# Seven block products instead of eight for the values and gates of a retention layer, inside a two-layer decoder trunk

## The chip, the cores and the metric

The kernel runs on one core of a Trainium2 chip. Times are device microseconds of one execution, the median of several runs where not said otherwise; the profile is of one profiled execution. TensorE does the matrix products, VectorE, ScalarE and GpSimd the elementwise work, and SyncE issues the transfers. In the profile these are PE (PEld its weight loads), DVE, ACT, POOL and SP.

## The reference

A residual stream `h` of 1024 tokens by 1024 features passes two layers. Everything is float32.

```python
u = rms_norm(x, ret_norm_pre)
q, k, v, g = split(u @ ret_w_in)          # 4 heads: q, k of 256, v, g of 512 features
q, k = rope(q), rope(k) / 16
o = retention(q, k, v)                    # o_t = sum_{s<=t} gamma_h^(t-s) (q_t.k_s) v_s
o = (o - mean(o)) * rsqrt(var(o) + EPS)   # per head and token
h = x + rms_norm((o * silu(g)) @ ret_w_out, ret_norm_post)
k2, v2 = split(rms_norm(h, kv_norm) @ w_kv)          # 8 heads: k of 128, v of 256
q2, g2 = split(rms_norm(h, sb_norm_pre) @ sb_w_in)
o2 = stick_breaking_attention(q2, k2, v2)
out = h + rms_norm((o2 * silu(g2)) @ sb_w_out, sb_norm_post)
```

## The kernel before

**Layout.** Features lie on the 128 partitions, tokens along the free side. The tokens are worked through in two halves of 512. `run()` (L691) goes through four phases: retention on half 0 and half 1 (A, t = 0 and 1), then attention on half 0 and half 1 (C). Each phase has four units: the retention heads, or pairs of attention heads. The state of each retention head after half 0 goes through DRAM (`st_d`) to half 1; keys and values of attention half 0 do too.

**Precision.** Each float32 operand is split in two parts of a reduced matmul type: a rounded copy (ScalarE) and the remainder (VectorE). A product is then three matmuls, high by high, high by low and low by high (`mm3`, L114). An operand of activations is 128 x 2 x 512 (`hl`).

**Weights.** They lie in DRAM as units of 128 x 1024 (512 KB). `unit` (L91) loads one into a raw tile `wraw` (three buffers), copies it (L107) and subtracts (L108) into `whl` (three buffers). Where a gain belongs to it, L110 and L111 do that with the gain of the norm as a scale. A projection (`proj`, L119) of 1024 features by 512 columns takes 4 units and 96 matmuls: 8 row blocks, 4 PSUM banks, 3 matmuls each; a unit serves 24 matmuls. Type "N" leaves features on the partitions (q, k), type "V" keeps the tokens' block as the stationary operand and streams the weights, so that tokens are on the partitions (v, g).

**One retention unit** (`AHead`, L289): the projection of q and k, in which the previous head's gate is done as side steps; the output projection of the previous head (`outproj`, L145); the projection of v, with the scores as side steps; the projection of g, with the mix as side steps (scores times v, plus the state; normalised per token; `mix`). The `rope` step (L278) reads each of the four banks of q and k twice on VectorE, adds on GpSimd and splits. The pre-norm factor of each token isn't applied to x: x is split with the gain only (L255, L256), the sums of squares run beside it, and the factor is put into the cosine and sine tables, into a scale of v (L303, L307, L308) and of g (L317, L318).

**What becomes of y.** The output projection sums over the heads: `y` lives in SBUF as eight tiles of 128 x 512, each chunk copied (first head, L164) or added (L166), and with the last head squared and summed (`sumsq`, L185, its additions on GpSimd at L191). `a_post` (L418), which runs as side steps of the next phase's first two units, takes the row of factors, scales y, adds x, splits h and stores it twice: in split form (`hh_d`) and whole (`h_d`). `c_prep` loads the split form for the attention phases; there too the token factor is multiplied in after the projections (L487 for keys and queries, L505 for values, L516 for gates), and the gate's last multiplication is on GpSimd (L518). `c_post` scales y, adds h (into a table tile of two buffers) and stores the result; `finish` is the last output projection of the kernel, with the closing norm.

**The order of the work.** `merge` (L172) deals the side steps out among the chunks of a projection; a scheduler then sets the order on each engine, and pools of tiles with a fixed number of buffers bring the waits. PSUM has eight banks: four "mm" (projections), two "z" (scores, transposes, sums), two "o" (mix, first two chunks of a retention output projection). All transfers are issued by SyncE (L61), in one queue that runs in order.

## Time and profile before

| | before |
|---|---|
| median of three runs | 1817.19 us (1815.28, 1817.19, 1819.95) |
| profiled execution | 1819.82 us, span 1818.0 us, mean TensorE clock 0.993 |
| busy TensorE, VectorE, ScalarE, GpSimd | 1767.5, 1038.1, 724.1, 308.6 us |
| bytes moved by DMA | 208.09 MB, 114 GB/s on average |
| retention half 0, half 1 (last addition to y of each) | 0 to some 442 us, then to some 875 us |
| attention half 0, half 1 | then to some 1293 us, then to the end |

A row of groups reads: line, engine, operation, output <- inputs, shapes, count, then busy us and mean ns of one, then the idle time of its engine just before and what ended it. A row of windows reads: the stretch in us, its length, and for PE, PEld, DVE, ACT and POOL the busy us with the number of instructions, then the TensorE clock granted, the DMA share and GB/s. A matmul's busy time is not the spacing of matmuls, since they overlap. A row of waits reads: engine and line that waited, what released it, us in all, times, longest.

### The profile page before, as it was taken

Reading aid. Unit: us, or ns where it says so; the run is one execution under the profiler, and the core shown is the slowest. Engines: PE = TensorE matmul, PEld = TensorE weight load, DVE = VectorE, ACT = ScalarE, POOL = GpSimd, SP = SyncE. Lnnn points to the kernel's source line nnn. Section 1 sums busy time; section 2 is a strip of 40 time slices with the busy share of each in tenths; the row PEclk is TensorE's granted clock in tenths of the full one; section 3 lists DMA queues with packets and bytes.
Section 4 is the critical chain, followed back from the end, with each engine's and each line's share of the span. In section 5 each row is a group of like instructions: output and inputs, shape, how many; then the busy total and the mean of one; then the engine's idle time right before and its main releaser. Section 6 shows DMA issues by size and latency. Waiting matters only on the chain.

```text
span 1818.0 us, 21852 instructions
## 1 busy us (share of the span) xinstructions
PE 1767.5 (97%) x8290; PEld 1466.5 (81%) x8290; DVE 1038.1 (57%) x1588; ACT 724.1 (40%) x1288; POOL 308.6 (17%) x376
## 2 busy tenths in 40 slices
PE   7999999999899999999999999999998999999987
PEld 6888888888788888888877888888876887887876
DVE  7363454564945363545596465556586446756665
ACT  4343323353333232323454343443444434444441
POOL 4110010113431010111122120201212012101123
PEclk9999999999999999999999999999999999999999
DMA  5222222343362232243364423354244232222321
GB/s 175 82 94 92 93 82 92 108 158 105 136 212 93 70 105 92 83 147 108 116 245 172 140 72 127 115 180 133 99 133 134 87 105 93 92 82 91 108 79 49
DMA packets 66376, 208.09 MB, mean 114 GB/s; under 512 B 7520, under 2 KB 9696, under 8 KB 66272
## 3 DMA queue, kind: packets, MB, share of 16 engines
q1 hardware_dynamic: 66272, 206.70, 33.9%
q8 instruction: 65, 1.06, 0.2%
q14 instruction: 39, 0.32, 0.1%
HBM read 173.12 MB, written 33.55 MB: 114 GB/s over the span
## 4 chain that ended last, share of the span: by engine, by line
PE 71%; issue 17%; DVE 7%; POOL 2%; DMA 2%; ACT 1%; SPq 0%; POOLq 0%; DVEq 0%; ACTq 0%
PE pmm L115 19%; PE pmm L117 19%; PE pmm L116 19%; PE po L117 3%; PE po L116 3%; PE po L115 3%; DVE sgn L550 2%; DMA tab<-h 1%; DVE whl L111 1%; PE pz L117 1%; PE pz L116 1%; PE pz L415 1%; PE pz L115 1%; PE pz L575 1%; DVE A L551 1%
## 5 line engine op out<-in xcount | busy, mean ns | idle before, releaser
L108 DVE TENSOR_TENSOR whl<-wraw,whl 128x1024 fp32r<-128x1024 f32 (+1 forms) x158 | 196.6, 1246 | 217.6 <-ACT whl L107 217.3
L115 PE MATMUL pmm<-xh,whl 128*128 128x512 f32 x768 | 308.3, 401 | 11.5 <-ACT whl L107 7.3
L115 PE MATMUL pmm<-whl,xh 128*128 128x512 f32 x768 | 302.1, 394 | 4.1 <-DVE v L308 2.7
L117 PE MATMUL pmm<-xh,whl 128*128 128x512 f32 x768 | 301.9, 393 | 0.7 <-DVE whl L108 0.7
L116 PE MATMUL pmm<-xh,whl 128*128 128x512 f32 x768 | 300.9, 392 | 0.0
L116 PE MATMUL pmm<-whl,xh 128*128 128x512 f32 x768 | 300.3, 391 | 0.0
L117 PE MATMUL pmm<-whl,xh 128*128 128x512 f32 x768 | 300.3, 391 | 0.0
L107 ACT ACTIVATE whl<-wraw 128x1024 fp32r<-128x1024 f32 (+1 forms) x158 | 165.3, 1047 | 237.9 <-PE pmm L117 225.6
L111 DVE SCALAR_TENSOR_TENSOR whl<-wraw,gn,whl 128x256 fp32r<-128x256 f32 (+1 forms) x256 | 153.2, 639 | 103.5 <-ACT whl L110 103.0
L110 ACT ACTIVATE whl<-wraw,gn 128x256 fp32r<-128x256 f32 (+1 forms) x256 | 143.7, 608 | 148.7 <-PE pmm L117 111.0
L115 PEld LDWEIGHTS pmm<-xh,whl 128*128 128x128 f32 x768 | 145.3, 189 | 41.4 <-ACT whl L107 7.3
L115 PEld LDWEIGHTS pmm<-whl,xh 128*128 128x128 f32 x768 | 144.9, 189 | 34.1 <-DVE v L308 2.9
L117 PEld LDWEIGHTS pmm<-xh,whl 128*128 128x128 f32 x768 | 144.8, 189 | 33.5 <-DVE whl L108 1.7
L117 PEld LDWEIGHTS pmm<-whl,xh 128*128 128x128 f32 x768 | 144.7, 188 | 30.8
L116 PEld LDWEIGHTS pmm<-whl,xh 128*128 128x128 f32 x768 | 145.0, 189 | 28.3
L116 PEld LDWEIGHTS pmm<-xh,whl 128*128 128x128 f32 x768 | 145.3, 189 | 26.6
L548 POOL TENSOR_SCALAR_AFFINE_SELECT sgn<-sgn 128x128 f32<-128x128 f32 x64 | 24.9, 389 | 638.8 <-ACT sgn L543 603.0
L115 PE MATMUL pmm<-oT,whl 128*128 128x512 f32 x336 | 132.9, 395 | 0.0
L117 PE MATMUL pmm<-oT,whl 128*128 128x512 f32 x336 | 131.5, 391 | 0.0
L116 PE MATMUL pmm<-oT,whl 128*128 128x512 f32 x336 | 131.4, 391 | 0.0
L550 DVE TENSOR_TENSOR_SCAN sgn<-sgn 128x128 f32<-128x128 f32 (+3 forms) x64 | 92.7, 1448 | 58.8 <-POOL sgn L548 58.8
L191 POOL TENSOR_TENSOR acc<-acc,f 128x512 f32<-128x512 f32 x49 | 74.4, 1522 | 147.5 <-ACT f L190 146.6
(182 smaller groups left out, 2822.5 us busy)
## 6 DMA issues: line engine op xcount, KB each, us to landing
wraw<-in_wts_dram SPq DMA_DIRECT2D x254, 512.0 KB, 3.3
xh<-hh SPq DMA_DIRECT2D x16, 512.0 KB, 3.7
v<-v SPq DMA_DIRECT2D x16, 512.0 KB, 3.2
vo<-v SPq DMA_DIRECT2D x32, 256.0 KB, 3.2
st<-ko SPq DMA_DIRECT2D x8, 512.0 KB, 3.6
vo<-in_xT_dram SPq DMA_DIRECT2D x16, 256.0 KB, 5.1
ko<-st SPq DMA_DIRECT2D x8, 512.0 KB, 3.9
h<-y SPq DMA_DIRECT2D x16, 256.0 KB, 2.7
```

The source lines that it names most:

```text
L107: A_.activation(w[:, 0, a:b], raw[:, a:b], AF.Copy)
L108: V.tensor_tensor(w[:, 1, a:b], raw[:, a:b], f32(w[:, 0, a:b]), ALU.subtract)
L110: A_.activation(w[:, 0, a:b], raw[:, a:b], AF.Copy, scale=g)
L111: V.scalar_tensor_tensor(w[:, 1, a:b], raw[:, a:b], g, f32(w[:, 0, a:b]), ALU.mult, ALU.subtract)
L115: MM(p, lh, rh, start=start, stop=False)
L116: MM(p, lh, rl, start=False, stop=False)
L117: MM(p, ll, rh, start=False, stop=stop)
L191: G.tensor_tensor(acc[:], acc[:], t[:], ALU.add)
L415: nc.tensor.transpose(pt[:, 128 * e:128 * e + 128], on[:, 128 * e:128 * e + 128], ident[:])
L548: G.affine_select(n[:, dg], n[:, dg], [[-1, 128]], ALU.is_gt, 1.0, base=0, channel_multiplier=1)
L550: V.tensor_tensor_scan(n[:, :W][:, ::-1], n[:, :W][:, ::-1], n[:, :W][:, ::-1], 1.0, ALU.mult, ALU.bypass)
L551: V.tensor_tensor(a[:, :W - 1], a[:, :W - 1], n[:, 1:W], ALU.mult)
```

## The change

**Seven products.** For one head and one half, v and g are [v g] = x W with W of 1024 by 1024 and x of 512 tokens. Cut into two by two blocks (two token halves of 256, two feature halves of 512 on the one side; v and g on the other) this is eight block products and four sums. The new `vg` computes it in seven products, with four sums of blocks on either side and a few on the results (a Strassen-Winograd form). The blocks of x are combined once per half (`sums`, four operands `T`, split like x); the blocks of W are combined for each head in `left`: 16 raw units are loaded instead of 8, and 14 are split, of which 8 are sums or differences first made on VectorE in place or in a new tile `S` (two buffers). A unit serves 12 matmuls. The products accumulate in two pairs of banks, `ma` and `mb`: a product may continue on the bank of the one before it (`goes_on`), after that has been copied to an SBUF tile (`copy`, ScalarE) or added to such a copy (`plus`, VectorE). This is done for every head of both halves but the first of half 0, which keeps two projections, v from x without the token factor (`first_v`) and g from normed x.

**Norm first.** x and h are multiplied by the token factor before they are split, so rotary tables, v, g and all attention evacuations lose their factor. `a_stats` takes the statistics of half 1 during half 0 (steps `pre`, dealt out at u = 2 and again at u = 3 of the first phase). In attention the gate's last multiplication moves from GpSimd to VectorE, reading PSUM.

**y in DRAM.** Each chunk of an output projection loads its y from DRAM, adds and stores it (`y_d`). `a_post` stores h once, whole; `c_prep` loads that, multiplies and splits. `a_post` is moved from the first unit of the next retention phase to its second and third. `f2` has six buffers instead of five, the scores have tiles of their own, and the four "mm" banks are two `ma` and two `mb`, which projections and output projections take in the order `banks4`.

```diff
-    BUFS = dict(xh=8, y=8, tab=2, wraw=3, whl=3, qk=4, v=4, vo=4, oT=4, A=5, sgn=2, AT=3,
-                ko=2, sg=4, row=1, f2=5, acc=2, small=24, col=8, mm=4, z=2, o=2)
+    BUFS = dict(xh=8, tab=2, wraw=3, whl=3, S=2, qk=4, v=4, vo=4, oT=4, A=5, sgn=2, AT=3,
+                ko=2, sg=4, f2=6, acc=2, small=24, col=8, sc0=1, sc1=1, sc2=1, sc3=1, ma=2, mb=2, z=2, o=2)
+    banks4 = ("mb", "mb", "ma", "ma")
...
-                box["p"] = PS(tag if c < 2 else "mm")
+                box["p"] = PS(tag if tag and c < 2 else banks4[c % 4])
+                box["y"] = S("f2", [512])
+                if not first:
+                    dma(box["y"][:], y_d[c])
...
-                V.tensor_tensor(y[c][:], p[:], y[c][:], ALU.add)
+                V.tensor_tensor(y[:], p[:], y[:], ALU.add)
+            dma(y_d[c], y[:])
...
+            V.scalar_tensor_tensor(src, src, gcol(G_PRE, k), X.row[:], ALU.mult, ALU.mult)
+            x = X.xh[k] = hl("xh")
+            split((x[:, 0, :], x[:, 1, :]), src)
...
+            V.tensor_tensor(a[:, 0], q[1], q[0], ALU.subtract)
+            V.tensor_tensor(a[:, 1], q[3], a[:, 0], ALU.subtract)
+            V.tensor_tensor(b[:, 0], q[3], q[1], ALU.subtract)
+            V.tensor_tensor(b[:, 1], q[2], a[:, 1], ALU.subtract)
...
+            def left(n, i):
+                s = box["S"]
+                if n == 1:
+                    src = load(0, i)
+                elif n == 2:
+                    src = load(0, 2 + i)
+                elif n == 5:
+                    a, b = load(1, i), load(1, 2 + i)
+                    src = s[i] = S("S", [1024])
+                    V.tensor_tensor(src[:], a[:], b[:], ALU.add)
+                elif n == 6:
+                    a, src = load(0, i), s[i]
+                    V.tensor_tensor(src[:], src[:], a[:], ALU.subtract)
+                elif n == 3:
+                    src = load(0, 2 + i)
+                    V.tensor_tensor(src[:], src[:], s[i][:], ALU.subtract)
+                elif n == 7:
+                    a, src = load(1, 2 + i), s[i]
+                    V.tensor_tensor(src[:], a[:], src[:], ALU.subtract)
+                else:
+                    src = load(1, 2 + i)
+                w = S("whl", [2, 1024], F32R)
+                split((w[:, 0, :], w[:, 1, :]), src[:])
+                return w
...
+            order = [(n, i) for n in (1, 2, 5, 6, 3, 7, 4) for i in range(2)]
...
+                banks = box["be"] if n in (2, 5, 3) else box["al"]
+                first = n in (1, 2, 5)
+                for tb in range(2):
+                    xh, xl = right(n, kt, tb)
+                    cl = slice(512 * kk, 512 * kk + 512)
+                    mm3(banks[tb][:], xh, xl, w[:, 0, cl], w[:, 1, cl], first and kt == 0, kt == 3, goes_on=not first)
+                if kt < 3:
+                    return
+                for tb, p in enumerate(banks):
+                    if n in (1, 5, 6):
+                        box[n, tb] = copy(p)
+                    elif n == 2:
+                        self.vput(tb, plus(box[1, tb], p), cc[:, 4 * h + tb:4 * h + tb + 1])
+                    elif n == 3:
+                        self.vput(2 + tb, plus(box[6, tb], p), cc[:, 4 * h + 2 + tb:4 * h + 3 + tb])
+                    elif n == 7:
+                        self.gput(2 + tb, plus(box[5, tb], p))
+                    else:
+                        self.gput(tb, p[:])
...
-                    merge(H.vproj(), (H.scores(), 7, 0), (post3[0] if u == 0 else post3[3] if u == 1 else [], 0, 0))
-                    merge(H.gproj(), (H.mix(), 3, 0), (post3[1] if u == 0 else [], 4, 0))
+                        merge(held if u < 3 else held[:4], (pre if u == 2 and nxt[0] == "A" else post[:4] if u == 1 else post[6:9] if u == 2 else pre, 0, 2 if u < 3 else 0))
...
+                    mix = H.mix()
+                    n = 3 if t else 2
+                    side = [(H.scores(), 7, 11), (mix[:n], 14, 6), (mix[n:n + 2], 23, 0)]
+                    if u in (1, 2):
+                        side.append((post[4:6] if u == 1 else post[9:], 4, 8))
+                    merge(H.vg(), *side)
+                    rest = mix[n + 2:]
```

More of the change, by code (lines that the diff above doesn't have):

```diff
@@ new lines, in stat1, with a_stats, sq, col @@
+        def stat1():
+            tables()
+            first.col = rstd_col(first.acc)
+        def stat2():
+            X.row = keep_row(first.col)
+        return X, first, [lambda k=k: load(k) for k in range(8)], \
+            [stat1, stat2] + [lambda k=k: norm(k) for k in range(8)], [lambda i=i: sums(i) for i in range(4)]
+    def a_stats(t):
+        box = {}
+        def sq(i):
+            raw = a_load(t, i, "wraw")
+            A_.activation(raw[:], raw[:], AF.Square)
+            if i == 0:
+                box["acc"] = S("acc", [512])
+                G.tensor_tensor(box["acc"][:], raw[:, 0:512], raw[:, 512:1024], ALU.add)
+            else:
+                for c in range(2):
+                    G.tensor_tensor(box["acc"][:], box["acc"][:], raw[:, 512 * c:512 * c + 512], ALU.add)
+        def col():
+            box["col"] = rstd_col(box["acc"])
+        def row():
+            rowh[0] = keep_row(box["col"])
+        return [lambda i=i: sq(i) for i in range(4)] + [col, row]
@@ L325, in scores, with out @@
+        def out(self, y_d, acc=None):
+            return outproj(self.base + 12, self.oT, y_d, self.h == 0, acc, "o")
         def scores(self):
@@ L639, in prep, with fetch @@
             hs.append(a)
+        def fetch():
+            for ng in range(4):
+                f = S("oT", [2, 512])
+                for b in range(2):
+                    dma(f[:, b], y_d[2 * ng + b])
+                    y.append(f[:, b])
         def chunk(th, c):
@@ L747, in run @@
                     last = P
-            acc = S("acc", [512])
             if kind == "A":
-                side = (last.gate(), 1, 4)
+                side = (rest + last.gate(), 1, 4)
             else:
```

335 lines of the change are left out of this document (195 added, 140 removed).

## The prediction

> **What bounds the kernel now.** First the page's list of engines and its chain of waits: where is the end set?
>
> ```profile
> span 1818.0 us, 21852 instructions
> PE 1767.5 (97%) x8290; PEld 1466.5 (81%) x8290; DVE 1038.1 (57%) x1588; ACT 724.1 (40%) x1288; POOL 308.6 (17%) x376
> PE 71%; issue 17%; DVE 7%; POOL 2%; DMA 2%; ACT 1%; SPq 0%; POOLq 0%; DVEq 0%; ACTq 0%
> ```
>
> TensorE is busy 97% of the span, VectorE 57%. Busy is not the price of a matmul, though. The grouped rows give the busy mean, the timeline of TensorE the spacing:
>
> ```profile
> L116 PE MATMUL pmm<-xh,whl 128*128 128x512 f32 x768 | 300.9, 392 | 0.0
> 300.22 0.39 PE L117 MATMUL pmm<-whl,xh 128*128 128x512 f32 x1
> 300.45 0.39 PE L115 MATMUL pmm<-whl,xh 128*128 128x512 f32 x1
> ...
> 309.29 0.39 PE L115 MATMUL po<-v,vo 128*128 128x512 f32 x1
> 317.45 0.60 PE L415 MATMUL pz<-ident,sgn 128*128 128x128 f32 x4
> ```
>
> Each matmul shows 0.39 us, but they overlap: from the one at 300.22 to the one at 309.29 lie 40 of them, all of this width, 9.07 / 40 = 0.2268 us from start to start. So a removed 512-wide matmul returns 0.2268 us, not 0.392. (Four 128-wide transposes take 0.60, 0.15 each.) The Trainium skill, Perfetto Trace Analysis, section Identifying the Most-Contended Engine, says the same: matmul busy time is a poor measure as matmuls overlap, and the weight loads' share is the better one; here that is 81% against 97%.
>
> Next, windows of the four phases, where idle time of TensorE would show (columns: window, us, then PE, PEld, DVE, ACT, POOL busy, TensorE clock, DMA share, GB/s):
>
> ```profile
> 0.00:10.00 10.00, 2.69 (x6) 2.10 (x7) 3.29 (x8) 4.91 (x8) 1.22 (x5) 1.00 0.65 198
> 100.00:200.00 100.00, 100.00 (x466) 83.09 (x465) 42.10 (x66) 36.98 (x61) 10.68 (x16) 1.00 0.27 89
> 490.00:500.00 10.00, 4.47 (x17) 3.29 (x16) 10.00 (x12) 2.95 (x5) 4.17 (x4) 0.80 0.60 184
> 970.00:980.00 10.00, 8.10 (x28) 6.68 (x29) 2.94 (x6) 0.66 (x2) 0.00 (x0) 0.66 0.76 286
> 1500.00:1600.00 100.00, 97.90 (x456) 80.48 (x456) 67.04 (x86) 46.51 (x87) 16.18 (x20) 1.00 0.28 90
> ```
>
> In most of a retention half TensorE never idles; its holes are at the start (7 us), where the post of a half stands in the first unit of the next (5.5 us near 490, with VectorE full; 1.9 near 970, with a clock of 0.66) and some 2% of the attention halves. Retention is a pure matmul count, so matmuls taken out there pay in full, as long as what feeds them keeps up.
>
> **The change, part by part.** *Matmuls.* Seven of the eight (head, half) units run 7 x 2 x 12 = 168 matmuls of 512 for values and gates instead of 192: 7 x 24 = 168 fewer. 168 x 0.2268 = **-38.1 us**. (By busy means it would be -65.7; I don't take that.)
>
> *What feeds them.* A weight unit used to carry 24 matmuls (5.44 us), now 12 (2.72 us), and 8 of the 14 are first combined on VectorE. Prices:
>
> ```profile
> wraw<-in_wts_dram SPq DMA_DIRECT2D x254, 512.0 KB, 3.3
> L107 ACT ACTIVATE whl<-wraw 128x1024 fp32r<-128x1024 f32 x154 | 163.0, 1058 | 237.0 <-PE pmm L117 225.6 <-issue 8.4 <-PE po L117 2.8
> L108 DVE TENSOR_TENSOR whl<-wraw,whl 128x1024 fp32r<-128x1024 f32 x154 | 193.6, 1257 | 217.3 <-ACT whl L107 217.0
> 469.40 1.93 DVE L108 TENSOR_TENSOR whl<-wraw,whl 128x1024 fp32r<-128x1024 f32 x1
> 477.60 1.21 DVE L108 TENSOR_TENSOR whl<-wraw,whl 128x1024 fp32r<-128x1024 f32 x1
> 478.74 3.11 DVE L438 SCALAR_TENSOR_TENSOR y<-y,gn,row 128x512 f32<-128x512 f32 x3
> L166 DVE TENSOR_TENSOR y<-pmm,y 128x512 f32<-128x512 f32 x76 | 52.1, 686 | 51.3 <-PE pmm L117 51.3
> L308 DVE SCALAR_TENSOR_TENSOR v<-pmm,small,v 128x512 fp32r<-128x512 f32 x32 | 22.7, 749 | 15.6 <-ACT v L307 15.6
> ```
>
> A 1024-wide subtraction occupies VectorE 1.14 us (477.60 to 478.74), 1.26 by the mean, 1.93 beside GpSimd work. One vg stage needs 14 splits + 8 combinations = 22 x 1.14 = 25.1, 6 additions of a copied product and 8 evacuations at some 0.63 = 8.8, and the splits of the scores (1280 columns) and of the first outputs, some 4.9 (an estimate from 0.69 per 512 columns): 38.8 us; with the mean durations 45. TensorE has 168 x 0.2268 = 38.1 there (by chance the saving's number too), and as side steps 24 score matmuls of 320 columns on average (3.4), 16 transposes (2.4) and 30 matmuls of the mix (6.8): 50.7 us. So VectorE runs at 77 to 89% and TensorE still leads. A unit's chain, 3.3 + 1.26 + 1.06 + 1.26 = 6.9 us, starts one unit ahead and three raw buffers deep; it is hidden in the mean, not at each handoff: the second load of product 5 and the load of product 7 can only be issued when a raw buffer comes free, with some 3 us to spare before their unit is due.
>
> The Trainium skill, SBUF — State Buffer, section Who interferes with whom, states that a VectorE instruction with two SBUF inputs contends with a GpSimd one that reads SBUF; the 1.93 against 1.21 above agrees, and speaks against this change, whose combinations all have two SBUF inputs. By it, were all eight combinations of a stage to meet one, VectorE would have 8 x 0.72 = 5.8 us more, 44.6 of 50.7: an estimate that leaves the sum alone and feeds the slower rival's chance.
>
> Direct waits stay in each stage: product 5 takes the bank pair of product 2, and product 4 continues on the pair of product 7, so TensorE waits until an addition (0.69) has read the bank. The later bank's own three matmuls (0.68) hide about half: 0.5 to 1 us each. I take 2 us a stage, **+14** over seven; lower end 0, upper end 6 a stage (VectorE at its mean durations, each handoff late).
>
> *Banks.* The rotary step now leaves k in "ma", and chunk 2 of the output projection asks for "ma" first; before, it got the first bank freed.
>
> ```profile
> L280 DVE TENSOR_TENSOR f<-pmm,tab 128x512 f32<-128x512 f32 x16 | 10.9, 679 | 1.0 <-PE pmm L117 1.0
> 462.31 0.69 DVE L280 TENSOR_TENSOR f<-pmm,tab 128x512 f32<-128x512 f32 x1 [0.98 <-PE pmm L117]
> 462.91 0.68 DVE L281 TENSOR_TENSOR f<-pmm,tab 128x512 f32<-128x512 f32 x1
> ```
>
> That bank is free after six reads, 6 x 0.60 = 3.6, with two splits of 1.14 and a delay between: some 6.7 us, while chunks 0 and 1 last 24 x 0.2268 = 5.4. Six times 1.2 = **+7** (0 to 12).
>
> *Norms first.* In each half x is multiplied by its row before the split (8 more instructions like L308, 6 us) and the operands for the new products cost 16 subtractions of 256 and 8 splits (some 6 + 6). In the first half these lie beside TensorE work, with VectorE busy 42 us in 100 (the window 100 to 200): nothing, except that head 0 starts with one whole 512 KB unit instead of two halves and waits for the statistics: **+3** (0 to 6). The statistics of the second half come early (a_stats), but its list is issued at u = 2 and again at u = 3 of the first half: two rounds of 7 GpSimd additions ahead of the rotary step's own two:
>
> ```profile
> L191 POOL TENSOR_TENSOR acc<-acc,f 128x512 f32<-128x512 f32 x49 | 74.4, 1522 | 147.5 <-ACT f L190 146.6
> L284 POOL TENSOR_TENSOR f<-f,f 128x512 f32<-128x512 f32 x16 | 20.8, 1299 | 186.5 <-DVE f L282 186.5
> ```
>
> 7 x 1.52 = 10.7 us each; a rotary addition behind half of that holds q and k back, and through k the scores: **+4** in all (0 to 10). The hole near 490, 5.5 us and a clock of 0.80, goes with the post that is moved out of that unit; but at the seam itself, near 440, normalising and sums come due: with the weight splits and the additions of y I count 44 to 50 us of VectorE against 168 matmuls and the gate's transposes, 44.6 us, of the last output projections. I take **-3** for both (-6 to +6).
>
> *y in DRAM.* Each output chunk loads y, adds, stores; h is no longer stored split. In the built programs SP's list grows from 454 to 737 DMAs, all in one queue, which already stands waiting most of the time:
>
> ```profile
> SPq L61 <- DVE whl L108: 577.7, 116, 13.5
> SPq L61 <- POOL y L439: 13.9, 6, 4.8
> h<-y SPq DMA_DIRECT2D x16, 256.0 KB, 2.7
> vo<-in_xT_dram SPq DMA_DIRECT2D x16, 256.0 KB, 5.1
> L439 POOL TENSOR_TENSOR y<-y,vo 128x512 f32<-128x512 f32 x8 | 11.5, 1458 | 14.9 <-DMA vo<-in_xT_dram 8.6 <-DVE y L438 6.3
> ```
>
> The y load is issued with its chunk, 12 matmuls or 2.7 us before the addition, and the scheduler may pull it ahead by the six f2 buffers: hidden, but if late its 2.7 us (the h store's, same size) holds a bank, not yet TensorE, since three more stand ready. In the second half the post of the first moves to u = 1 and 2, beside vg; an h store that waits for GpSimd's addition (up to 4.8 us before) has weight loads behind it, which a 12-matmul unit covers only with 2.7. Twice 2 = **+4** (0 to 12).
>
> *Attention halves.* The row and column factors are gone: 32 VectorE multiplications for gates and 32 for keys and queries (0.67 each) less, and 32 GpSimd ones (1.73) are now VectorE's.
>
> ```profile
> L516 DVE TENSOR_TENSOR f<-pmm,tab 128x512 f32<-128x512 f32 x32 | 20.7, 674 | 0.8 <-PE pmm L117 0.8
> L518 POOL TENSOR_TENSOR sg<-f,sg 128x512 f32<-128x512 f32 x32 | 54.7, 1725 | 22.4 <-ACT sg L517 22.4
> L115 PE MATMUL pmm<-xh,whl 128*128 128x512 f32 x768 | 308.3, 401 | 11.5 <-ACT whl L107 7.3 <-DVE f L516 3.3 <-DVE v L505 0.7
> L621 DVE TENSOR_TENSOR y<-y,tab 128x512 f32<-128x512 f32 x8 | 5.5, 688 | 13.2 <-DMA tab<-h 13.2
> ```
>
> TensorE waited 3.3 + 0.7 us for the old evacuations; with the post no longer bound to two table buffers (13.2 us of idle in VectorE's stream) I take **-5** (0 to -10), and **+1** for the fetch of y before the last output projection.
>
> Sum: -38.1 + 14 + 7 + 3 + 4 - 3 + 4 - 5 + 1 = **-13.1 us**. The profiled execution took 1819.8 (span 1818.0 and 1.8 around it), 2.6 above the median of the three runs, 1817.2; so 1806.7 for it, **1804** by the median. What can't be told from no change is about 0.3%, 5.5 us.
>
> **The rivals.** *Full gain.* Handoffs in vg hide behind the scores and mix steps, banks come free in time: -38.1 + 7 (one us a stage) + 3 - 3 - 5 + 4 = -32, so 1785. For it: VectorE at 76%, ACT at 40%. Against: two bank waits per stage that no cover stands beside.
>
> *VectorE sets the pace of vg.* Where a combination meets GpSimd (1.93 instead of 1.14) and ACT's turn lies between two of VectorE's, each unit takes 1.93 + 1.06 + 1.26 = 4.3 us against 2.72 of matmuls and 0.9 of side steps. A loss of 6 us a stage makes 42 instead of 14: -13.1 + 28 = +15, so 1832. It decides from (13.1 + 14) / 7 = 3.9 us a stage. Against: GpSimd was active 11 us in 100 in this half.
>
> *One queue.* The order on SP delays the weight units behind y and h stores: two more us in each of the seven stages eat the gain: about 1818, no change. For it: SP waits 578 us for raw buffers, and they are drawn twice as fast; against: those waits cost TensorE 11.5 us in all.
>
> By the Trainium skill's VectorE: DVE Perf Modes, section Why `tensor_tensor` can't do 2×_2P or 4×, a two-tensor fp32 instruction has no faster mode; the 1.14 to 1.26 us per 1024 agrees, so nothing makes the combinations cheaper than the sum has them.
>
> **How the numbers follow.** Forecast (faster, 1795 to 1811) 0.40, full gain 0.17, one queue 0.15, VectorE as the bound 0.28. Faster 0.57, same 0.15, slower 0.28. The range reaches from the full gain with a little more from the seams, 1782, to VectorE's pace, 1834; the likeliest case alone has 1795 to 1811.
>
> **What would show it.** Right: TensorE has about 168 fewer matmuls at the same 0.2268 spacing; windows of a retention half show it at 94 to 97 of 100 instead of 100, with the holes at product 5 and product 4 (released by the addition L449) and at chunk 2 of the output projection (released by the rotary L280 to L283 lines); VectorE's busy time near 1220 us, some 80% inside vg; GpSimd below 300. Wrong: holes before every unit, released by VectorE's split or combination, or windows with VectorE at 95 (the slower rival); raw loads that land late while VectorE idles (the queue); a TensorE clock below 1.00 in the retention halves, which my sum doesn't hold; or a seam near 440 that grows beyond 10 us since norms and sums come due there.

## The result

The changed kernel is slower: 1832.31 us (median of four runs, 1828.78 to 1835.83) against 1816.69 us of the kernel before in the same comparison, a ratio of 1.0083 with a 95% interval of 1.006 to 1.0107. That is some 15 us more where the forecast had 13 less. The profiled execution has a span of 1834.1 us. Ratios, here and below, leave out three executions that took far longer than all others (2198, 2900 and 9932 us).

The page of the changed kernel, engines and chain of waits:

```profile
span 1834.1 us, 22500 instructions
PE 1753.6 (96%) x8132; PEld 1438.4 (78%) x8132; DVE 1185.7 (65%) x1776; ACT 798.6 (44%) x1404; POOL 291.7 (16%) x345
issue 30%; PE 12%; DVE 7%; DMA 4%; POOL 2%; ACT 1%; SPq 0%; POOLq 0%; DVEq 0%; ACTq 0%
```

The instruction counts are those that were foreseen: 158 TensorE instructions fewer (168 products less, a few more for the statistics), VectorE at 1186 us for 1038 (near 1220 was foreseen), GpSimd a little lower. But the chain of waits gives TensorE 12% where it gave 71%, and leaves over 40% of the span to nobody, so it can't be read for the cause; the gaps of TensorE can.

To see where TensorE lost the time, take every matmul from its timeline and sum what the distance to the next start exceeds 0.2268 us per 512 columns. The matmuls themselves are worth 36.7 us less than before. The lost time rose by 53 us: in the two retention halves from 30 to 91, in the two attention halves it fell from 70 to 62. Of the 91 some 51 stand at a named wait, and 40 in matmuls that are slow without one. The waits of TensorE, longest groups (what waited, what released it, us in all, times, longest):

```profile
PE pmb L120 <- ACT whl L110: 6.9, 1, 6.9
PE pz L219 <- DVE sgn L215: 6.7, 6, 2.0
PE pmb L120 <- DVE f L449: 6.5, 5, 2.5
PE pz L581 <- DVE oT L226: 5.8, 4, 2.8
PE pma L120 <- DVE f L449: 5.1, 4, 2.2
PE po L120 <- ACT sgn L564: 4.6, 1, 4.6
PE pma L120 <- ACT f L171: 3.6, 1, 3.6
```

The first row is the start of the kernel, which waits for its first weights; L215 builds a row of token factors. L449 is the addition of a copied product, L226 at `oT` the split of the gate, L564 the normalisation of the mix, L171 the copy of a first output chunk. They are late for a reason one step further back. Two examples, with their timelines, and what a wait costs beside its own length:

*A bank held by an addition that stands behind a late load.* TensorE and VectorE of the changed kernel around 717 us, third head of half 1, product 2 to product 5:

```profile
716.79 0.39 PE L122 MATMUL pz<-qk,qk 128*128 128x512 f32 x1
719.69 0.74 PE L120 MATMUL pmb<-whl,A 128*128 128x512 f32 x1 [2.51 <-DVE f L449]
720.23 0.63 PE L121 MATMUL pmb<-whl,A 128*128 128x512 f32 x1
720.65 0.63 PE L122 MATMUL pmb<-whl,A 128*128 128x512 f32 x1
...
713.19 1.23 DVE L420 TENSOR_TENSOR S<-wraw,wraw 128x1024 f32<-128x1024 f32 x1 [2.49 <-DMA wraw<-in_wts_dram]
715.60 1.22 DVE L226 TENSOR_TENSOR whl<-S,whl 128x1024 fp32r<-128x1024 f32 x1 [1.19 <-ACT whl L225]
717.71 1.23 DVE L420 TENSOR_TENSOR S<-wraw,wraw 128x1024 f32<-128x1024 f32 x1 [0.88 <-DMA wraw<-in_wts_dram]
718.85 1.28 DVE L449 TENSOR_TENSOR f<-pmb,f 128x512 f32<-128x512 f32 x2
```

VectorE isn't full here: it idles 2.49, 1.19 and 0.88 us. It stands in order before the combination L420, whose raw units come late, and the two additions that free product 2's banks are behind it, at 718.85. The wait for the load just before them is 0.88 us; a split (1.22) and the combination (1.23) stand in front of them too, so lateness and VectorE's own work both have a part in the 2.51 us.

*A matmul stream that restarts at half speed.* In the same lines the matmuls after the wait start at 720.23 and 720.65, 0.42 us apart, where 0.2268 is normal. A wait costs twice, once by itself and once in the slow stretch behind it. The windows of the changed kernel show it in the granted clock (third number from the end):

```profile
580.00:600.00 20.00, 16.41 (x61) 13.01 (x60) 7.25 (x8) 8.10 (x13) 6.71 (x6) 0.83 0.79 268
640.00:660.00 20.00, 17.45 (x65) 13.88 (x66) 12.63 (x21) 7.30 (x10) 2.42 (x6) 0.83 0.42 144
```

An estimate of such stretches from the mean clock: 1834.1 x (1 - 0.987) = 23.8 us, and 1818.0 x (1 - 0.993) = 12.7 before, 11 us more. It is rough, as the record of the clock doesn't always go with the pace: in the kernel with eight products below it has a mean of 0.941, and the 512-wide matmuls keep a median spacing of 0.227 us. The Trainium skill, TensorE: Matmul & The Clock Gate, Part 1: The HAM clock gate, gives an idle window of some 3.4 us, free-running, as the condition for half rate; here a hole of 2.5 us was enough.

*A post whose load holds ScalarE.* ScalarE, GpSimd and TensorE of the changed kernel at 580 to 592 us, second head of half 1, with the post of half 0 beside it:

```profile
583.83 0.60 ACT L171 ACTIVATE f<-pma 128x512 f32<-128x512 f32 x1 [0.46 <-PE pma L122]
590.07 0.63 ACT L609 ACTIVATE vo<-vo 128x512 f32<-128x512 f32 x1 [5.64 <-POOL vo L604]
590.61 0.58 ACT L171 ACTIVATE f<-pma 128x512 f32<-128x512 f32 x1
...
588.78 1.26 POOL L604 TENSOR_TENSOR vo<-vo,vo 128x512 f32<-128x512 f32 x1 [5.47 <-DMA vo<-in_xT_dram]
...
587.26 0.39 PE L121 MATMUL pma<-whl,xh 128*128 128x512 f32 x1
591.24 0.79 PE L120 MATMUL pma<-whl,xh 128*128 128x512 f32 x1 [3.59 <-ACT f L171]
```

The copy of an output chunk (0.58 us) waits behind the post's square, that for GpSimd's addition, and that for a load of x: 3.6 us of TensorE, and an estimated 2.6 more for the clock.

### The profile page after: what moved, and what is told of

It reads as the page before. It is cut to its first block, busy times and chain, and to the rows that moved or that the text cites. A ratio compares the mean times of both kernels' runs of the same rounds, so it can differ in the third digit from the quotient of the medians.

```text
span 1834.1 us, 22500 instructions
## 1 busy us (share of the span) xinstructions
PE 1753.6 (96%) x8132; PEld 1438.4 (78%) x8132; DVE 1185.7 (65%) x1776; ACT 798.6 (44%) x1404; POOL 291.7 (16%) x345
## 4 chain that ended last, share of the span: by engine, by line
issue 30%; PE 12%; DVE 7%; DMA 4%; POOL 2%; ACT 1%; SPq 0%; POOLq 0%; DVEq 0%; ACTq 0%
DMA f<-y 2%; PE pma L120 2%; PE pma L121 2%; PE pma L122 2%; PE pmb L121 1%; PE pmb L122 1%; PE pmb L120 1%; DVE sgn L713 1%; POOL A L712 1%; DVE f L173 1%; POOL sgn L711 1%; DVE whl L226 1%; DMA wraw<-in_wts_dram 1%; DVE A L714 1%; PE po L122 1%
## 5 line engine op out<-in xcount | busy, mean ns | idle before, releaser
L111 DVE TENSOR_TENSOR whl<-wraw,whl 128x1024 fp32r<-128x1024 f32 (+1 forms) x102 | 130.1, 1279 | 106.9 <-ACT whl L110 106.8
L120 PE MATMUL pmb<-xh,whl 128*128 128x512 f32 x384 | 153.8, 401 | 7.0 <-DVE f L173 3.5
L120 PE MATMUL pma<-xh,whl 128*128 128x512 f32 x384 | 155.4, 405 | 5.1 <-DVE sg L681 2.8
L122 PE MATMUL pma<-xh,whl 128*128 128x512 f32 x384 | 151.1, 393 | 0.0
L121 PE MATMUL pma<-xh,whl 128*128 128x512 f32 x384 | 150.6, 392 | 0.0
L121 PE MATMUL pmb<-xh,whl 128*128 128x512 f32 x384 | 150.5, 392 | 0.0
L122 PE MATMUL pmb<-xh,whl 128*128 128x512 f32 x384 | 150.4, 393 | 0.0
L110 ACT ACTIVATE whl<-wraw 128x1024 fp32r<-128x1024 f32 (+1 forms) x102 | 106.1, 1041 | 101.3 <-PE pma L122 72.8
L120 PE MATMUL pmb<-whl,xh 128*128 128x512 f32 x256 | 100.8, 395 | 1.1 <-DMA wraw<-in_wts_dram 1.1
L121 PE MATMUL pmb<-whl,xh 128*128 128x512 f32 x256 | 99.8, 390 | 0.2 <-DVE whl L226 0.2
L122 PE MATMUL pmb<-whl,xh 128*128 128x512 f32 x256 | 99.8, 390 | 0.0
L226 DVE TENSOR_TENSOR AT<-pz,AT 128x512 fp32r<-128x512 f32 (+1 forms) x96 | 52.6, 554 | 69.6 <-ACT AT L225 69.3
L226 DVE TENSOR_TENSOR whl<-wraw,whl 128x1024 fp32r<-128x1024 f32 x56 | 74.6, 1336 | 28.1 <-ACT whl L225 27.3
L120 PEld LDWEIGHTS pmb<-xh,whl 128*128 128x128 f32 x384 | 72.6, 189 | 23.3 <-DVE f L173 4.5
L120 PEld LDWEIGHTS pma<-xh,whl 128*128 128x128 f32 x384 | 72.7, 189 | 23.0 <-DVE sg L681 6.7
L225 ACT ACTIVATE whl<-wraw 128x1024 fp32r<-128x1024 f32 x56 | 59.3, 1058 | 62.5 <-PE pma L122 17.6
L122 PEld LDWEIGHTS pma<-xh,whl 128*128 128x128 f32 x384 | 72.6, 189 | 16.2
```

The costliest lines, as they stand in the source:

```text
L110: A_.activation(w[:, 0, a:b], raw[:, a:b], AF.Copy)
L111: V.tensor_tensor(w[:, 1, a:b], raw[:, a:b], f32(w[:, 0, a:b]), ALU.subtract)
L120: MM(p, lh, rh, start=start, stop=False, **kw)
L121: MM(p, lh, rl, start=False, stop=False, **kw)
L122: MM(p, ll, rh, start=False, stop=stop, **kw)
L225: A_.activation(dst[0], src, AF.Copy)
```

## The experiments

Three theories were set against each other. A: the seven products pay, the rest of the change (statistics, posts, y in DRAM) loses more. B: the seven products can't be fed and cost more than they save. C: the one transfer queue, or y's traffic in it, is at fault. Each kernel was compared with the kernel before on its own chip; a ratio is to that, and the changed kernel's is 1.0083. Differences between two kernels by their ratios are good to some 4 us; 0.001 is 1.8 us.

### Eight products with the rest of the change

```diff
-                    merge(H.vg(), *side)
+                    merge(H.v8() + H.first_g(), *side)
```

> Values and gates are projected in eight products again (two projections, from normed x; the sums of x fall away); statistics, posts, y in DRAM and the attention half stay as changed. Theory A, the seven products still pay by themselves and the rest of the change loses the time: of 38.1 us saved some 14 go into bank waits, 7 into late weight units and 5 into the slower clock after them, 12 remain, so this kernel is slower than the changed one, 1844 us. Theory B, the seven products can't be fed and cost more than they save: this kernel is faster than the changed one, 1825 us or less. Theory C, the one transfer queue is at fault: with 8 weight loads less per head and twice the time for each the queue is relieved, 1832 us or less.

Measured 1839.92 us, ratio 1.0112 (1.0097 to 1.0127): 5 us slower than the changed kernel. So the seven products do pay, but some 5 (good to 4) of the 38.1 us that the count of matmuls gives; and without them the rest of the change costs 20 us. A, with less left over than expected.

### Statistics once

```diff
-... else post[6:9] if u == 2 else pre, ...
+... else post[6:9] if u == 2 else [] if nxt[0] == "A" else pre, ...
```

> The statistics of the second half are taken once (third head), not again with the fourth. Theory A: the second round stands for holes of TensorE of 4.2 us at 331 to 338 and 2 us near 354 with a slower clock behind the first: 7 us less, 1825 us. Theory B: these holes are only moved, 1832 us, within 2. Theory C: four 512 KB loads less in the queue, 3 us less.

Measured 1828.22 us, ratio 1.0049 (1.0034 to 1.0064): 6 us less, as A had it. What in the second round costs them is not shown: ScalarE's wait for x on its way through the raw weight buffers falls from 16.4 us to 12.7, and the statistics through the S tiles, further on, take that wait away and gain nothing. The wait in the changed kernel:

```profile
ACT wraw L334 <- DMA wraw<-in_xT_dram: 16.4, 7, 4.2
```

### The post's addition on VectorE

```diff
-            (V if t else G).tensor_tensor(y[:], y[:], raw[:], ALU.add)
+            V.tensor_tensor(y[:], y[:], raw[:], ALU.add)
```

> In the post of half 0 the addition of x goes from GpSimd to VectorE, as it is for half 1. Theory A: the hole of 4.7 us at 637, where the normalisation waits behind such an addition on GpSimd, and part of that of 3.8 us at 587 go, with 2.6 us of slow clock behind each: 8 us less, 1824 us. Theory B: VectorE is the bound of these stages and gets 8 x 0.69 us more: 4 us more, 1836 us. Theory C: the h stores wait for less, 3 us less.

Measured 1831.34 us, ratio 1.0066 (1.0049 to 1.0083): 3 us less by the ratios, within what can't be told. The hole at the normalisation (L564) and that at the copy of an output chunk (L171) are gone from the trace; the retention halves lose 84.7 us in place of 91.0, while the waits of projections for VectorE's f tiles (additions of products and of y, rotary step) grew from 18 to 25 us. A wait that was taken away came back in part at the next one.

### No y traffic

```diff
-                if not first:
-                    dma(box["y"][:], y_d[c])
...
-                V.tensor_tensor(y[:], p[:], y[:], ALU.add)
-            dma(y_d[c], y[:])
+                V.tensor_tensor(y[:], p[:], f32(oT[0][:, 0, :]), ALU.add)
             if acc is not None:
+                dma(y_d[c], y[:])
```

> Work left out: y isn't summed over the heads; an output chunk adds an SBUF tile that is there already, loads no y, and only the last head of a phase stores its chunk. All other work is kept. Theory A: holes released by the additions of y and its copies (4 + 4.5 us in the retention halves, 2 in attention) and clock behind them: 8 us less, 1824 us. Theory B: 2 us less. Theory C, the queue sets the pace: at least 16 us less, 1816 us or below.

This kernel leaves out the sum of y over the heads, so its result isn't the layer's; it does without 184 transfers of 256 KB, 48 MB. Measured 1814.45 us, ratio 0.9971 (0.996 to 0.9982): 20 us less than the changed kernel, and 5 less than the kernel before. This is the largest part that a single run takes away, and what C said. The raw weight units land in 3.3 us without the traffic and in 3.6 with it (last column; first the changed kernel, then this one):

```profile
wraw<-in_wts_dram SPq DMA_DIRECT2D x310, 512.0 KB, 3.6
```

```profile
wraw<-in_wts_dram SPq DMA_DIRECT2D x310, 512.0 KB, 3.3
```

### No y traffic, eight products

```diff
-                    dma(box["y"][:], y_d[c])
...
-                    merge(H.vg(), *side)
+                    merge(H.v8() + H.first_g(), *side)
```

> Work left out as in the kernel without y traffic (y isn't summed over the heads, not loaded, stored only by the last head), and eight products in place of seven. Theory A: the seven products keep their own price of waits, so the difference of this kernel to the one without y traffic (1814) is what it was with the traffic, 5 to 6 us: 1820. Theory C: the traffic of y slowed the weights of the seven products above all; without it they are worth 15 or more: 1829 or above.

Measured 1827.45 us, ratio 1.0067 (1.0041 to 1.0094), 13 us above the run without y traffic by the medians and 17 by the ratios. So the seven products are worth 13 to 17 us when y isn't in the way, and 5 when it is: C, in that the traffic of y costs more beside the seven products. Some 8 to 12 of y's 20 us are this; with eight products y costs only the other 8 to 12. With neither, the kernel is still 8 to 12 us slower than the kernel before.

### y a chunk ahead

The rows that suggested it: VectorE's last two additions of y in half 0, and SyncE's issues between them, in the changed kernel.

```profile
460.99 0.69 DVE L173 TENSOR_TENSOR f<-pma,f 128x512 f32<-128x512 f32 x1 [0.67 <-DMA f<-y]
464.88 0.69 DVE L173 TENSOR_TENSOR f<-pma,f 128x512 f32<-128x512 f32 x1 [3.19 <-DMA f<-y]
...
461.71 0.32 SPq L63 DMA_DIRECT2D y<-f  x1
462.08 0.42 SPq L63 DMA_DIRECT2D f<-y  x1
```

The load of the next chunk is issued behind the store of the last, which waits for the last addition: 3.9 us a chunk.

```diff
-                box["y"] = S("f2", [512])
-                if not first:
-                    dma(box["y"][:], y_d[c])
+                for k in range(0 if c == 0 else c + 1, min(c + 2, 8)):
+                    box[k] = S("f2", [512])
+                    if not first:
+                        dma(box[k][:], y_d[k])
```

> The load of y for an output chunk is issued one chunk earlier, with the chunk before it; bytes, number and queue of the transfers stay. Theory C1, the order in the one queue is what y in DRAM costs: the load stands behind the store of the previous chunk, which waits for the previous addition, so that a chunk takes addition, store, load and landing, 4.2 to 4.5 us, against 2.7 of matmuls; with the load ahead most of the 20 us that the kernel without y traffic gained come back: 1819 us on the scale where the changed kernel has 1834. Theory C2, it is the bytes and the number of transfers (the DMA engines are shared): no gain, 1834, within 3.

Measured 1834.52 us, ratio 1.0101 (1.0077 to 1.0126): no gain. The edit did what it should: VectorE's wait for y fell from 36.4 us to 11.6 (first the changed kernel, then this one), and the time stayed. Taken away alone, that wait was not what y costs.

```profile
DVE f L173 <- DMA f<-y: 36.4, 18, 4.5
```

```profile
DVE f L174 <- DMA f<-y: 11.6, 8, 2.6
```

### y's transfers on ScalarE's queue

```diff
-                    dma(box["y"][:], y_d[c])
+                    dma(box["y"][:], y_d[c], nc.scalar)
...
-            dma(y_d[c], y[:])
+            dma(y_d[c], y[:], nc.scalar)
```

> The changed kernel with all loads and stores of y in the output projections issued by ScalarE's queue, not SyncE's; bytes and number stay. Theory C1: the place of y's transfers among the weights in the one in-order queue is what costs: 10 us less or more, 1824. Theory C2: it is their bytes on the shared DMA engines: 1834, within 3. Against either: ScalarE then waits in order for the additions, which holds up its copies; slower than 1838 would say that this wait is the larger one.

Measured 1839.18 us, ratio 1.012 (1.0104 to 1.0135): 7 us slower. That ScalarE waits in order for the additions may hide a gain, so this settles only that the other queue is no remedy.

### Statistics through the S tiles

```diff
-            raw = a_load(t, i, "wraw")
+            raw = a_load(t, i, "S")
```

(with the statistics once)

> The statistics of the second half are taken once, and x for them is loaded to the S tiles, which are free between the products, and not to the raw weight buffers. Theory A: ScalarE stood waiting for these loads with the gate's copies queued behind it (holes of TensorE near 219 and 227); 5 us less than with the statistics taken once (1828): 1823. Theory B: the holes come from ScalarE's and VectorE's load and stay: 1828.

Measured 1831.41 us, ratio 1.0081 (1.0053 to 1.011): no gain over the statistics taken once (3 us more by the medians, 6 by the ratios). ScalarE's wait for x is gone from the trace, and the time isn't. The holes at the gate did shrink, others grew: between the first two stages of seven products TensorE loses 6.1 us where it lost 12.5, in the first stage 5.9 for 1.6 and in the third 10.2 for 6.7.

### Three edits together

```diff
+                for k in range(0 if c == 0 else c + 1, min(c + 2, 8)):    # y a chunk ahead
+            raw = a_load(t, i, "S")                                   # statistics once, through S
+            V.tensor_tensor(y[:], y[:], raw[:], ALU.add)              # the post
```

> All three together: y loaded a chunk ahead, the statistics once and through the S tiles, the addition of the post of half 0 on VectorE. If the causes are separate and the order of the queue is what y costs (A with C1): 1834 - 15 - 11 - 2 = 1806, faster than the kernel before (1819). If y costs by its bytes (C2): 1821.

Measured 1818.26 us, ratio 1.0008 (0.9993 to 1.0024): 14 us less than the changed kernel, level with the kernel before. Whether the three give more together than singly can't be told: by the ratios the runs that made them (the load ahead, the statistics once through S, the addition) add up to nothing, each good to some 4 us, but by the spans of the profiled executions (2, 6 and 6 us less than the changed kernel) to the same 14. No run has two of them without the third at the same addresses, so what the load ahead gives beside the others is open too.

### Pools: f2 and raw buffers

Four raw weight buffers for three, f2 with five tiles for six to make room, alone and with the statistics once, through S, and the post on VectorE; then seven f2 tiles, alone and with all three edits; then five f2 tiles without y traffic.

```diff
-                ... wraw=3, ... f2=6, ... small=24 ...
+                ... wraw=4, ... f2=5, ... small=20 ...     (or f2=7)
```

> The changed kernel with four raw weight buffers for three (room made by f2 with 5 tiles for 6). Theory A2: in the vg stages VectorE stands in order before the combination of product 5's second unit, which waits for its two loads, and the addition that frees the bank of product 2 comes behind it (holes of 1.5 to 2.7 us, with half clock after them); with a fourth buffer these loads land earlier: 6 to 10 us less, 1826 us where the changed kernel has 1834. Theory B2: these holes come from VectorE's own load in the stage: 1834, and up to 3 more for the f2 tile.

> Four raw buffers as before this run, with the statistics once and through the S tiles and the addition of the post of half 0 on VectorE; y is loaded with its chunk. With A2 the gains add: 1818 (the three together, y a chunk ahead) - 6 = 1812. With B2: 1820 or more.

> The changed kernel with seven f2 tiles for six, and nothing else. Theory F, the pool of f2 tiles is short because y's tiles stay taken while their loads and stores are in flight: 6 us less or more, 1828 us or below where the changed kernel has 1833. Theory C2, the bytes: 1833, within 3; then the 12 us of the kernel with four raw buffers came from these and not from the f2 tile.

> The combination (statistics once and through the S tiles, y a chunk ahead, the addition of the post on VectorE) with seven f2 tiles. Theory F: the load ahead holds two tiles, so a seventh gives more here than alone: 8 us less than the combination, 1810. Theory C2: 1818, within 3.

> Work left out as in the kernel without y traffic (y isn't summed over the heads, not loaded, stored only by the last head), with five f2 tiles for six. Theory F: without transfers a tile of y is taken for one addition only, so the fifth does as well: 1814, within 4. If five tiles are too few for the rotary step and the copies themselves, y or not: 12 us more, 1826.

Measured 1845.9 (ratio 1.0149, 1.0134 to 1.0164), 1841.85 (1.013, 1.0108 to 1.0151), 1848.03 (1.0162, 1.0146 to 1.0177), 1828.12 (1.0056, 1.0041 to 1.0071) and, without y traffic, 1815.53 us (0.9986, 0.9977 to 0.9996). Of the first four, which have 20 small tiles and one constant less, three are slower than either theory had them; the fifth, with 24, isn't. In the records of all four some 350 to 380 of the 512-wide matmuls more than in the changed kernel are spaced at 0.24 to 0.3 us. The 20 small tiles had moved all tiles laid out after them, among them x, v and the scores, from multiples of 512 bytes to 384 bytes above one. So these runs say nothing of the pools; three more do.

```diff
-                ... small=24, col=8 ...
+                ... small=20, col=8 ...
```

> The changed kernel with 20 small tiles for 24 and nothing else: the tiles laid out behind them start 384 bytes above a multiple of 512, not on it. Theory G, the address of a matmul's operand sets its spacing: some 1000 of the 512-wide matmuls go from 0.227 to 0.24 or more, 20 us more, 1853 us. If it was the pool sizes: 1833, within 3.

Measured 1845.27 us, ratio 1.0151 (1.0132 to 1.017): 12 us more than the changed kernel. The four tiles less are not missed: what TensorE loses at named waits didn't grow (71 us, 75 in the changed kernel), what it loses without one did (101 for 84). So it is the address. The same 48 matmuls of an attention projection, first and last, in the changed kernel and then in this one:

```profile
1044.59 0.39 PE L120 MATMUL pmb<-whl,xh 128*128 128x512 f32 x1
...
1055.24 0.39 PE L122 MATMUL pma<-whl,xh 128*128 128x512 f32 x1
```

```profile
1052.27 0.39 PE L120 MATMUL pmb<-whl,xh 128*128 128x512 f32 x1
...
1063.18 0.40 PE L122 MATMUL pma<-whl,xh 128*128 128x512 f32 x1
```

47 spacings take 10.65 us, 0.2266 each, with x on a multiple of 512 bytes, and 10.91 us, 0.2321 each, off it. The matmuls of the output projection, whose operands were not moved, kept their spacing (0.229 to 0.230 us on average in both).

```diff
-                ... f2=6 ...
+                ... f2=7 ...     (or wraw=4, f2=5)
-    ident = sb.tile([128, 128], F32, name="ident")
-    ones = sb.tile([128, 128], F32, name="ones")
+    ones, ident = f32(onesr[:]), f32(identr[:])
```

> Seven f2 tiles for six, with addresses as in the changed kernel (two constants of 128 x 128 are kept in one copy each). Theory F, y's tiles are short: 6 us less or more, 1827. Theory C2: 1833, within 3.

> Four raw weight buffers for three, five f2 tiles for six, with addresses as in the changed kernel. Theory A2, the loads for the combinations land late and VectorE stands in order before them, the bank's addition behind: 8 us less, 1825. Theory B2: 1833 or a little more for the f2 tile.

With the addresses on multiples of 512: 1833.85 us, ratio 1.0088 (1.0066 to 1.0111) with seven f2 tiles, and 1833.55 us, 1.0079 (1.0062 to 1.0096) with four raw buffers and five f2 tiles. Neither pool is what is short, within the 4 us that can be told. The fourth raw buffer didn't bring the loads earlier: the waits of the combination L420 (here L421) are as long as before (first the changed kernel, then this one). That points at the place of the load in SyncE's queue, but no run shows it.

```profile
DVE S L420 <- DMA wraw<-in_wts_dram: 14.4, 12, 2.5
```

```profile
DVE S L421 <- DMA wraw<-in_wts_dram: 15.9, 8, 4.0
```

### The attention half alone, on the kernel before

```diff
-                    f, g = S("f2", [512]), S("sg", [512])
-                    V.tensor_tensor(f[:], bg[b][:], self.X.rows[:], ALU.mult)
-                    A_.activation(g[:], f[:], AF.Sigmoid)
-                    G.tensor_tensor(g[:], f[:], g[:], ALU.mult)
+                    g = S("sg", [512])
+                    A_.activation(g[:], bg[b][:], AF.Sigmoid)
+                    V.tensor_tensor(g[:], bg[b][:], g[:], ALU.mult)
```

and likewise for keys, queries and values; `c_prep` loads h, norms and splits it; `a_post` stores h once; `c_post` takes f2 tiles. Retention, y in SBUF and the eight products are those of the kernel before.

> The attention half of the change alone, on the kernel before: h is stored once and whole, normed and split when it is loaded, evacuations without the row factor, the gate's product on VectorE, the closing post through f2 tiles; retention, y in SBUF and eight products as before. By the holes of TensorE the attention halves of the changed kernel lose 8 us less than before (62 against 70) although y goes through DRAM there; with y in SBUF 12 to 13 less: 1819 - 10 = 1809 us. If the gain came from the moved posts or from another place of work: 1819, within 3.

Measured 1802.11 us, ratio 0.9912 (0.9896 to 0.9929): 16 us faster than the kernel before and the fastest of all. Which of its edits gives how much isn't separated. The first 107 us of the last half, before and in this kernel (TensorE first):

```profile
1293.00:1400.00 107.00, 101.28 (x472) 82.48 (x471) 72.30 (x106) 46.73 (x93) 16.25 (x23) 1.00 0.38 120
```

```profile
1290.00:1397.00 107.00, 104.38 (x494) 85.90 (x493) 75.13 (x111) 49.67 (x99) 10.03 (x19) 1.00 0.40 131
```

TensorE gets through 494 instructions where it did 472. Waits of the transposes for a split fell from 11.2 to 5.2 us (first the kernel before, then this one), and VectorE's wait for h in the closing post, 13.2 us before, is gone. By the time lost between matmuls the attention halves go from 70 us to 50.

```profile
PE pz L575 <- DVE AT L217: 11.2, 6, 3.4
```

```profile
PE pz L571 <- DVE AT L218: 5.2, 3, 2.6
```

## Why the prediction was wrong

The forecast was 1804 us and faster; 1832 lies inside the range, and on its other side. In the forecast's own terms the retention halves were to lose 29 us more than before (14 + 7 + 3 + 4 - 3 + 4) and lost 61; the attention halves were to lose 4 less and lost 8 less; the matmuls came out as forecast. So the error lies in the waits of retention. Where it lies there, the timelines of five kernels show: the us that TensorE loses against 0.2268 us per 512 columns (one profiled execution each; the start of the kernel, 7 us, is in the last row). A stage goes from the first to the last product of values and gates, for the seven (head, half) units behind the first.

| | before | eight products, no y | eight products, y | seven, no y | changed |
|---|---|---|---|---|---|
| the seven stages | 14.4 | 17.9 | 23.9 | 33.5 | 52.1 |
| of these, the one beside the post of half 0 | 10.1 | 10.6 | 15.6 | 12.9 | 18.2 |
| between the first three stages | 2.1 | 16.9 | 20.0 | 19.4 | 16.5 |
| rest of the retention halves | 23.4 | 25.6 | 29.3 | 31.3 | 32.4 |

- **Matmuls, -38.1 us.** Right: the matmuls of the changed kernel are worth 36.7 us less by their columns, at the same spacing of 0.2268.
- **What feeds the products, +14 us, two a stage.** This step failed in size, together with the next. Against eight products the stages lose 28 us more, 4.0 a stage; without y's traffic 16, 2.2 a stage, which is what was forecast. In the first two stages, with neither statistics nor post beside them, it is 1.8 and 2.9 us even with the traffic. The step priced the two bank waits by the addition (0.69) that reads the bank; what it left out is that the addition stands in VectorE's order behind a combination that waits for its load, and that TensorE runs at half clock for some us after a hole of 2.5. The trace shows both; how much of the 28 is late weights and how much VectorE's own order isn't separated.
- **y in DRAM, hidden, with +4 for the posts.** This step failed: y's traffic alone is 20 us. For y it asked only whether a load lands before its addition. It often doesn't, 36 us of VectorE's time, but taking two thirds of that away, and nothing else, changed nothing. The cost is in what the 184 transfers do to the others: in the seven stages they cost 6 us with eight products and 19 with seven. Which part of it is bytes on shared DMA engines, and which the order of one queue, stays open: a load ahead, ScalarE's queue and more f2 tiles were tried one at a time and none gave it back.
- **Banks of the rotary step, +7.** Too high: TensorE's waits for L353 come to 1.3 us.
- **Statistics twice, +4.** Too low. Without the second round the time is 6 us less, and the loss between the second and the third stage falls from 6.6 to 1.0 us. Between the first two stages, where the first round stands, the changed kernel loses 9.9 us where the kernel before lost 1.0, and does so with eight products and without y too (9.8 to 13.4); no run ties that to one edit.
- **Attention halves, -5.** Too small: 16 us with y in SBUF.
- **The seam and the hole near 490.** The old hole (10.1 us of its stage) shrank, and new ones came with the posts near 590 and 640 (3.6 and 4.6 us of wait, and slow clock): the move didn't take the post's work away, it put it beside a stage with less cover, which loses 18.2 us, 10.6 even with eight products and no y. The forecast had the hole go.

The measured differences don't add up one by one: from the kernel with neither seven products nor y's traffic to the changed one it is 3 us by the ratios, 17 less for the products and 20 more for y, or 8 more for y and 5 less for the products, by the order in which they are taken. The rest of the 15 us stands in that kernel already, 12 us slower than before by the ratio although its attention halves lose 14 us less: its retention halves lose 21 us more, 15 of them between the first three stages.

Of the rivals, that of VectorE's pace had the time, 1832, and its threshold, 3.9 us a stage, was just passed (4.0 by the table); but its mechanism isn't what the trace shows. VectorE is busy for 70 to 91% of a stage, and at 80% in the first, where TensorE has no idle time (the last stage, at 91%, is near that rival's case). The first and the sixth stage of the changed kernel, where VectorE has much the same work (third busy time) and TensorE (first) idles for nothing and for 3.0 us:

```profile
144.00:192.50 48.50, 48.50 (x228) 39.50 (x228) 38.64 (x47) 26.97 (x38) 7.47 (x10) 1.00 0.53 184
703.90:760.60 56.70, 53.72 (x238) 43.93 (x238) 39.58 (x49) 24.96 (x33) 6.69 (x11) 0.97 0.53 186
```

The rival of the one queue was nearer: it gave the traffic two us a stage, and by the table it costs 2.7; whether by the queue's order isn't shown. The 11.5 us of waits that the prediction held against it contain one of 7.3 at the start of the kernel. The error of the sum was to price y and the products as if each had its own place: y was priced with the cover of the kernel before, where a unit lasts 5.4 us, and the products halve that cover. In the prediction's working, VectorE's 45 us a stage with mean durations come to 43 from the means shown, and the 44.6 us at the seam to 40.5 for the matmuls and transposes named; the sum doesn't rest on the first.

## What to carry to other kernels

Where fewer matmuls are bought with more loads, combinations and buffers, price the change by the time that one loaded unit covers, and ask for every wait which engine stands in order behind it: an addition of 0.7 us behind a split, a late load and a combination cost 2.5 us and the slow clock after it. Measure such a change in parts on the chip, and two parts that share a queue or a cover with and without each other: here a side part (the attention half) was worth 16 us alone, and keeping the sums in DRAM to make room cost 20 us, more than the 13 to 17 that the seven products give without it. When a pool's size is changed, keep the operands' addresses where they were, or an effect of the layout is read as one of the pool.

## What the runs showed of the hardware

A matmul with an operand 384 bytes above a multiple of 512 in SBUF was spaced 0.2321 us on average instead of 0.2266 (48 matmuls in a row), and a kernel that is otherwise the same but for four small tiles was 12 us slower; other offsets were not tried. After a wait of 2.5 us TensorE ran at half rate, 0.42 us a matmul, for some 3 us and after one of 3.6 us for some 5. The record of the granted clock had a mean of 0.941 in one execution (eight products) whose 512-wide matmuls kept a median spacing of 0.227 us, so that mean alone is no measure of lost time.
